# A decoder step on one Trainium2 core: the first half written in plain order, with a recorder in the kernel that orders its instructions and gathers TensorE's side products in 41 bursts

## The chip, the core and the metric

The kernel runs on one core of a Trainium2 chip. A core has TensorE (PE in the profile), VectorE (DVE), ScalarE (ACT), GpSimd (POOL) and SyncE (SP); here SP does little but issue DMAs. Each engine works through its own queue in the order in which the program was written; across engines, semaphores hold an instruction back until its data are there. The metric is the device time of one execution in microseconds, the median of the runs.

## The reference

One layer of a hybrid decoder for a prompt of 512 tokens and 8 samples of 4 tokens, which share all weights (width 1024):

```python
h = rmsnorm(x, norm_mix);  z = h @ w_in          # 3 x 512 columns of attention, 4 x 512 of HGRN
att = dilated_attention(aq, k_all, v_all)        # 8 heads of 64; the samples also read 2048 cached rows
f  = lb + (1 - lb) * sigmoid(hf)                 # HGRN: 4 heads of 128 x 128, a decaying state
S_t = f_t * S_(t-1) + outer(1 - f_t, hi_t);  o_t = S_t^T (silu(hq_t) / sqrt(128))
x += concat(head_rmsnorm(att), head_rmsnorm(o) * silu(hg)) @ w_out
c = rmsnorm(x, norm_cross)                       # cross attention: 4 heads of 128, 256 memory rows
x += softmax((c @ w_cq) k_mem^T / sqrt(128)) v_mem @ w_co
u = rmsnorm(x, norm_ffn)                         # feed forward, 2816 wide, causal convolution of 3
x += (silu(conv3(u @ w_gate)) * (u @ w_up)) @ w_down
y = rmsnorm(x, norm_final)                       # outputs: y, new k/v rows, HGRN states, conv rows, memory k/v
```

All of it is in fp32, for which the kernel uses split products (below).

## The kernel before

**Layout.** Activations lie with the channels on the 128 partitions and the N = 544 tokens (512 of the prompt, then 32 of the samples) in the free dimension, cut as `CUTS` says into 256 and 288. A weight block is 1024 x 128: eight tiles of 128 x 128 that PE holds while the tokens move past.

**Dense passes.** Weights and activations are each split into a high part (`wh`, `xmh`), which has the format fp32r, and the rest (`wl`, `xml`), so each k-tile costs three products: high by high, high by low, low by high. The product is that of L473 in `passes`; a pass over one cut has 24 of them (12 where only four k-tiles are summed, `ps_co`) and fills one of two PSUM banks `dense` (`PD`). ACT makes the high parts of a weight (L381), DVE the low parts (L390), one block ahead. DVE drains the bank (`evac`): `ps_q`, `ps_k`, `ps_v`, `ps_hf`, `ps_hq`, `ps_hg`, `ps_hv` of the input projection in the order `MIX_ORDER`, then `ps_ck` and `ps_cv` for the memory, `ps_wo`, `ps_cq`, `ps_co`.

**Side work.** What lies between dense passes is written as Python generators that a list, `Sides`, holds. A dense pass calls `between()` after half of its products and `sides.pump()` at its end; each pump advances every live generator to its next `yield`. So the hand-placed `yield` statements and the dense passes together set the order on all queues. The generators, with their PE products:
- `decode_attention`, the samples' attention to the 2048 cached rows: `psd` (scores, L719) and `psdo` (values, L770) read tiles `st` that a stream loads from SP's queue into five buffers; `qbd_win` holds the queries, `dpt` the transposed softmax (`psT` at L874). Each group of four products fills 32 of the array's columns and is repeated for four column groups. `pace()` and `PACE` say how many pumps lie between two stream tiles.
- `prompt_attention(p)`, for four pairs of heads: `pst_v` and `pss_v` (v by token, L679 and L684), then for each of four query blocks scores `psS` (L848), softmax on DVE and ACT, transposes `psT`, values `psO`.
- `hgrn(h)`, for four heads: seven levels of a pairwise scheme, in each of which DVE and POOL make operands `kq` from the gates `hf` and their running products `hG` (L922 makes the operand `hq`), and PE multiplies small blocks: `psB` and `psA` (32 x 32 blocks, L935), `psL` (L974, L979); then `psU`, `psu`, `psin` and `pso` for states and outputs, and `psr_hg` (L529) for the norm.
- `memory_in`, `cross_prompt` and `cross_sample` for the cross attention: scores `ps_cp` (L1375), transposes `ps_cpt`, values `ps_cpo`; for the samples `ps_cs`, `ps_cso` and, last, `ps_cos` (L1364), whose drain splits it into the last 32 columns of `coh` and `col`, the inputs of `ps_co`.

The norms between the parts need one product with a matrix of ones, `psr_...` (L529 in `rsqrt_rows`); `psr_cx` gives `r_cx`, by which the drain of `ps_cq` scales. Side products draw on five PSUM banks `aux` (`PX`) and one `dec` (`PDEC`); SBUF operands on a pool of equal slots (`A`).

**The rest.** From the end of `ps_co` on, the feed forward is ordered by `Plan`, a list scheduler in the kernel; the last pass `ps_dz` again by hand.

Of the kernel before, what the change touches and what calls it, by code (L numbers as in the profile page):

```python
# [16 lines left out]
D = 1024  # L17
SEQ = 512
# [39 lines left out]
PACE = (1, 1, 2)  # L58
# [3 lines left out]
HG_WAIT = (2, 0)  # L62
CO_EARLY = (2, 3)
# [17 lines left out]
for _n, _c in (("ident", 128), ("ones", 128), ("blk64", 128), ("dist", 512), ("lnc", 512), ("dbias", NR + 2 * NS),  # L81
               ("mask_a", 96), ("mask_b", 96), ("mask_s", 96), ("batch", NB), ("h8", 8), ("h4", 4), ("sel8", 16),
               ("sel4", 16), ("sel32", 32), ("own", 2)):
    _span(CST_COLS, _n, _c)
# [15 lines left out]
def _constants():  # L100
# [39 lines left out]
    put("batch", ((p[:32, None] // TS) == np.arange(NB)[None, :]).astype(np.float32))  # L140
# [112 lines left out]

@with_exitstack
def tile_decoder_step(ctx: ExitStack, tc: tile.TileContext, xT, memT, kwT, vw, s0, conv_in, mkT, mv, vecs, cst,
                      w_first, w_in, w_out, w_cq, w_ck, w_cv, w_co, w_gate, w_up, w_down,
                      yT, kT_out, vT_out, st_out, conv_out, mkT_out, mv_out, ss_out):
    nc = tc.nc
# [9 lines left out]
    def A(name, shape=None, dt=F32):  # L268
        return act.tile(shape or [128, FW], dt, tag="a", name=name, bufs=NA)

    def R(name):
        return act.tile([128, FW], F32R, tag="a", name=name, bufs=NA)[:, :N]

    def small(name, n=1):
        return one.tile([128, n], F32, tag=f"small{n}", name=name, bufs=16)

    def PD(name):
        return psum.tile([128, 512], F32, tag="dense", name=name, bufs=2)

    def PX(name):  # L280
        return psum.tile([128, 512], F32, tag="aux", name=name, bufs=5)

    def PDEC(name):
        return psum.tile([128, 512], F32, tag="dec", name=name, bufs=1)
# [13 lines left out]
    def step():  # L298
        flush()
        sides.pump()  # L300

    def leave(dst, src, wait=4):

        def gen():
            for _ in range(wait):
                yield
            nc.sync.dma_start(dst, src)
        sides.add(gen())

    vec = one.tile([128, NVEC], F32, name="vec")  # L310
    nc.scalar.dma_start(vec, vecs)
    mid = CST_COLS["dist"][0]
    cs = one.tile([128, mid], F32, name="cs")
    cs2 = strm.tile([128, NCST - mid], F32, name="cs2")
    eps = one.tile([128, 1], F32, name="eps")
# [29 lines left out]
    class Weights:  # L345
# [3 lines left out]
        def load(self, i, now=False):  # L349
            if i < len(specs) and i not in self.raw and (now or i < 3 or i - 3 in self.hl):  # L350
# [4 lines left out]
                if i < down_w:  # L355
                    t = wgt.tile([128, 8, 128], F32, tag="wraw", name=f"wr{i}", bufs=3)
                else:
                    t = A(f"wr{i}", [128, 4, 128])
# [6 lines left out]
        def split(self, i):  # L365
            if i < len(specs) and i not in self.hl:
                self.split_hi(i)
                self.split_lo(i)

        def split_hi(self, i):  # L370
            if i not in self.whole:
# [4 lines left out]
                else:  # L376
                    tiles = [(wgt.tile([128, 8, 128], F32R, tag="whi", name=f"wh{i}", bufs=2),
                              wgt.tile([128, 8, 128], F32R, tag="wlo", name=f"wl{i}", bufs=2), 0, k)]
# [15 lines left out]
        def take(self):  # L394
            self.load(self.i)
            self.split(self.i)
            return self.hl[self.i]

        def ahead(self):

            n = next(i for i in range(self.i, len(specs)) if i not in self.hl)
            for k in range(n + 1):
                self.load(k)
            self.split(n)
            for k in range(n, n + 4):
                self.load(k)

        def advance(self):

            for n in (1, 2, 3):  # L410
                self.load(self.i + n)
            self.split(self.i + 1)
            if self.i + 2 in resident:
                self.split(self.i + 2)
            self.i += 1
# [26 lines left out]
    class Stream:  # L442
# [3 lines left out]
        def load(self):  # L446
            if self.n < len(streams):
                src, w = streams[self.n]
                if self.n < len(streams) - LAST_MV:
                    t = strm.tile([128, 4, 256], F32, tag="st", name=f"st{self.n}", bufs=AHEAD)  # L450
# [18 lines left out]
    def passes(ps, w, xs, n0, n, order, between, first=True, last=True):  # L469
        for at, i in enumerate(order):  # L470
# [4 lines left out]
            if at == (len(order) + 1) // 2 - 1:  # L475
                between()

    def half(w, xs, name, evac, cut, order=None, advance=True):
        n0, n = cut
        ps = PD(f"ps_{name}_{n0}")  # L480

        def between():
            release()
            if advance:
                ws.advance()
            flush()
            if len(xs) > 4:
                sides.pump()

        passes(ps, w, xs, n0, n, order or range(len(xs)), between)  # L490
        evacs.append(lambda: evac(ps, n0, n))
        sides.pump()

    def dense(xs, name, evac, cuts=CUTS, after=None, order=None):
        w = ws.take()
        for c, cut in enumerate(cuts):
            half(w, xs, name, evac, cut, order, c == 0)
        if after is not None:
            pending.append(after)

    def dense_by_half(xs, count, name, evac, after=None, early=(), cuts=CUTS):

        held = []
        for c, cut in enumerate(cuts):
            for m in range(count):
                if c == 0:
                    held.append(ws.take())
                elif early and m in early:
                    ws.ahead()
                half(held[m], xs, f"{name}{m}", lambda ps, n0, n, m=m: evac(m, ps, n0, n), cut, None, c == 0)  # L510
                if after is not None:
                    pending.append(lambda m=m, c=c: after(m, c))
# [12 lines left out]
    def rsqrt_rows(acc, c0, c1, mat, width, r, name):  # L525

        for n0, m in ((c0, c1 - c0),) if c1 - c0 <= 512 else CUTS:
            ps = PX(f"psr_{name}_{n0}")
            nc.tensor.matmul(ps[:, :m], mat, acc[:, n0:n0 + m], start=True, stop=True)  # L529
            yield  # L530
            nc.scalar.activation(r[:, n0:n0 + m], ps[:, :m], AF.Ln, bias=eps, scale=1.0 / width)
            nc.scalar.activation(r[:, n0:n0 + m], r[:, n0:n0 + m], AF.Exp, scale=-0.5)

    def at_once(gen):
        for _ in gen:
            pass
        yield from ()
# [32 lines left out]
    for i in range(2):  # L570
        nc.scalar.dma_start(wf[i], w_first[i])
    nc.scalar.preload_act_table_set(LN_SET)
    for i in range(KT):
        if i == 0:
            x_load(i, 0, 256)
            x_load(i, 256, N)
        else:
            x_load(i, 0, N)
        if i > 1:
            nc.sync.dma_start(wf[i], w_first[i])  # L580
    nc.sync.dma_start(cs, cst[:, :mid])
    for i in range(3):
        ws.load(i)
    nc.sync.dma_start(cs2, cst[:, mid:])
    for _ in range(AHEAD - 1):
        stream.load()
    zero = A("zero")
    nc.vector.memset(zero[:, :128], 0.0)
    warm_up(WARM)

# [9 lines left out]

    for i in range(KT):
        hi, lo = A(f"wfh{i}", [128, 384], F32R), A(f"wfl{i}", [128, 384], F32R)
        for c0, c1 in ((0, 256), (256, N)) if i == 0 else ((0, N),):
            split_into(xs[i], xin[i][:, c0:c1], V("norm_mix", i), c0, c1)
            if c0 == 0:
                nc.scalar.copy(hi, wf[i])
                nc.vector.tensor_tensor(lo, wf[i], hi.bitcast(F32), op=ALU.subtract)
        wf_hl.append((hi, lo))
        if i > 1:
            square(i - 2)  # L610
        if i > 3:
            add_square(i - 3)
    square(KT - 2)
    add_square(KT - 3)
    square(KT - 1)
    add_square(KT - 2)
    add_square(KT - 1)
    ws.split(0)


    lbt = strm.tile([128, 4, 4], F32, name="lbt")
    l0 = vec[:, VEC_COLS["lb0"][0]:VEC_COLS["lb0"][1]]
    l1 = vec[:, VEC_COLS["lb1"][0]:VEC_COLS["lb1"][1]]
# [1333 lines left out]
```

## Time and profile before

| | |
|---|---|
| median of three runs | 864.36 us (864.08 to 864.73) |
| profiled execution | 866.38 us, of which the profile's span is 864.3 |
| TensorE's granted clock, mean | 0.996 of full |
| busy share of PE, DVE, ACT, POOL | 98%, 69%, 46%, 21% |
| DMA, mean over the span | 153 GB/s |
| products on PE | 7578 |

The table's shares are over the whole span. The part that the change rewrites ends at about 478 us; the feed forward fills what is left. PE's busy time is that in which at least one product is under way, and neighbouring products overlap, so a row's duration is more than the distance to the next row's start: what a product costs PE is read from distances between starts.

### The profile page before, as it was taken

To read this page: it belongs to the slowest core of one execution; us is meant where nothing else is said; L and a number is where in the kernel's file an instruction comes from. 1 tells how busy PE (TensorE), PEld (TensorE's weight loads), DVE (VectorE), ACT (ScalarE), POOL (GpSimd) and SP (SyncE) were. 2 spreads that over 40 slices of the span, in tenths; PEclk is the share of its full clock that TensorE was granted. 3 is DMA by queue.
4 is the path that set the end of the run, shared out by engine and by line. 5 is a ranking of instruction groups with operands and counts; after the bars stand their busy time and mean duration, and the time that the engine had idled before them with its cause. 6 is when DMAs were issued, how large, how long until landed. Compare 5 with 4: busy or idle time off the path is not lost.

```text
span 864.3 us, 18847 instructions
## 1 busy us (share of the span) xinstructions
PE 846.4 (98%) x7578; PEld 769.5 (89%) x7578; DVE 598.0 (69%) x1253; ACT 399.8 (46%) x796; POOL 177.2 (21%) x265
## 2 busy tenths in 40 slices
PE   9999999999999999999999999999999999999996
PEld 9997788877777776999888999999999999999995
DVE  6864246776787776546366689886877777777764
ACT  7422125245256334544445554654644544554533
POOL 0230000300300300122222214242322232232113
PEclk9999999999999999999999999999999999999999
DMA  8535875643762785423283227465565555555403
GB/s 303 174 120 145 263 216 177 187 137 101 253 211 76 255 283 186 119 74 110 86 248 103 74 74 175 131 159 135 146 156 138 139 143 151 144 135 134 130 28 104
DMA packets 90759, 132.32 MB, mean 153 GB/s; under 512 B 6064, under 2 KB 60080, under 8 KB 90544
## 3 DMA queue, kind: packets, MB, share of 16 engines
q1 hardware_dynamic: 84480, 120.69, 44.0%
q0 software_dynamic: 5184, 9.44, 6.8%
q8 instruction: 59, 0.97, 0.5%
q10 hardware_dynamic: 1008, 0.99, 0.3%
q14 instruction: 28, 0.23, 0.1%
HBM read 123.03 MB, written 8.07 MB: 152 GB/s over the span
## 4 chain that ended last, share of the span: by engine, by line
PE 83%; DVE 8%; issue 3%; ACT 3%; DMA 1%; POOL 1%; SPq 0%; DVEq 0%; POOLq 0%; ACTq 0%
PE ps_d L473 12%; PE ps_ag L1741 6%; PE ps_au L1741 6%; PE ps_wo L473 6%; PE ps_k L473 3%; PE ps_q L473 3%; PE ps_cg L1741 3%; PE ps_hv L473 3%; PE ps_cu L1741 3%; PE ps_dz L473 3%; PE ps_g L473 2%; PE ps_cq L473 2%; PE ps_hg L473 2%; PE ps_co L473 2%; PE ps_first L643 2%
## 5 line engine op out<-in xcount | busy, mean ns | idle before, releaser
L381 ACT CAST wh<-wr 128x1024 fp32r<-128x1024 f32 (+1 forms) x76 | 65.3, 874 | 82.7 <-PE ps_v L473 20.1
L390 DVE TENSOR_TENSOR wl<-wr,wh 128x1024 fp32r<-128x1024 f32 (+1 forms) x76 | 76.6, 1017 | 37.2 <-ACT wh L381 37.1
L1511 POOL TENSOR_TENSOR up<-up,cv 128x512 f32<-128x512 f32 x22 | 33.2, 1508 | 141.6 <-ACT up L1720 63.9
L956 POOL TENSOR_TENSOR hG<-hG,hf 128x256 f32<-128x256 f32 (+1 forms) x28 | 22.4, 800 | 140.5 <-DVE hf L919 77.3
L1236 DVE TENSOR_TENSOR xr<-xr,ps_d 128x256 f32<-128x256 f32 x80 | 34.7, 434 | 13.6 <-PE ps_d L473 12.7
L1498 DVE SCALAR_TENSOR_TENSOR cv<-ug,vec,cv 128x560 f32<-128x560 f32 x44 | 35.2, 800 | 3.9 <-ACT cv L1489 3.0
L859 ACT ACTIVATE P<-P,mx 128x128 f32<-128x128 f32 (+3 forms) x32 | 18.0, 561 | 39.6 <-DVE mx L858 39.6
L1493 POOL COPY last<-ug 128x2 f32<-128x2 f32 x22 | 11.5, 522 | 98.6 <-ACT ug L1720 80.6
L551 POOL TENSOR_TENSOR acc_cx<-acc_cx,sq_cx 128x256 f32<-128x256 f32 (+1 forms) x14 | 10.8, 771 | 90.1 <-ACT sq_cx L550 90.1
L1489 ACT ACTIVATE cv<-ug,vec 128x560 f32<-128x560 f32 x22 | 18.9, 858 | 16.4 <-DVE ug L1760 11.1
L958 DVE TENSOR_TENSOR hf<-hf 128x256 f32<-128x256 f32 (+1 forms) x28 | 14.5, 519 | 15.1 <-POOL hG L956 14.7
L856 DVE CUSTOM_DVE_ANT_0 P<-psS,bias 128x128 f32<-128x128 f32 (+3 forms) x32 | 15.5, 484 | 7.1 <-PE psS L848 7.0
L719 PE MATMUL psd<-st,qbd_win 128*32 128x224 f32 x256 | 18.7, 365 | 1.5 <-issue 1.5
L473 PE MATMUL ps_co<-coh,wh 128*128 128x256 f32 (+1 forms) x64 | 19.3, 301 | 0.9 <-DVE xr L1236 0.9
L1502 ACT ACTIVATE cv<-cv 128x560 f32<-128x560 f32 x22 | 14.8, 673 | 11.1 <-DVE cv L1498 10.4
L473 PE MATMUL ps_co<-col,wh 128*128 128x256 f32 (+1 forms) x64 | 18.4, 288 | 0.0
L473 PE MATMUL ps_co<-coh,wl 128*128 128x256 f32 (+1 forms) x64 | 18.4, 288 | 0.0
L770 PE MATMUL psdo<-st,dpt 128*32 128x256 f32 x224 | 17.9, 391 | 0.0
L657 DVE TENSOR_TENSOR k<-ps_k,r_mix 128x256 f32<-128x256 f32 (+1 forms) x8 | 3.5, 442 | 20.4 <-PE ps_k L473 20.4
L1754 ACT COPY keptrg<-ps_ag 128x272 f32<-128x272 f32 x9 | 3.5, 385 | 27.7 <-PE ps_ag L1741 27.7
L924 POOL MEMSET hG<- 128x544 f32 x4 | 2.2, 554 | 66.8 <-PE psO L889 33.4
L1687 DVE TENSOR_TENSOR wlu<-wru,whu 128x1024 fp32r<-128x1024 f32 x9 | 12.7, 1409 | 4.5 <-ACT whu L1681 4.5
(2671 smaller groups left out, 3622.3 us busy)
## 6 DMA issues: line engine op xcount, KB each, us to landing
st<-in_kwT SPq DMA_DIRECT2D x32, 448.0 KB, 3.8
st<-in_vw SPq DMA_DIRECT2D x28, 512.0 KB, 4.5
wr<-in_w_in SPq DMA_DIRECT2D x25, 512.0 KB, 4.5
wd<-in_w_down SPq DMA_DIRECT2D x32, 256.0 KB, 2.9
wrg<-in_w_gate SPq DMA_DIRECT2D x9, 512.0 KB, 5.8
wru<-in_w_up SPq DMA_DIRECT2D x9, 512.0 KB, 6.2
st<-in_mkT SPq DMA_DIRECT2D x8, 512.0 KB, 4.7
wr<-in_w_out SPq DMA_DIRECT2D x8, 512.0 KB, 4.0
```

The lines of the kernel that those rows point to most:

```text
L381: nc.scalar.copy(hi[:, :k1 - k0, :], raw[:, k0:k1, :])
L390: nc.vector.tensor_tensor(lo[:, :n, :], raw[:, k0:k1, :], hi[:, :n, :].bitcast(F32), op=ALU.subtract)
L473: nc.tensor.matmul(ps[:, :n], a, b[:, n0:n0 + n], start=(first and at == 0 and j == 0), stop=(last and at == len(order) - 1 and j == 2))
L719: nc.tensor.matmul(ps[32 * b:32 * b + 32, QUART * qu:QUART * qu + QUART], qbd[:, 4 * g + b, p, :], kt[b][:, :QUART], start=p == 0 and qu == 0,
L770: nc.tensor.matmul(po[32 * b:32 * b + 32, 256 * fh:256 * fh + 256], pts[ck // 4][:, at:at + 32], vs[b], start=ck == 0 and fh == 0, stop=ck ...
L859: nc.scalar.activation(pt[:, :nk], pt[:, :nk], AF.Exp, bias=mx, accum_out=den)
L956: nc.gpsimd.tensor_tensor(half(G, 0), half(G, 0), last, op=ALU.mult)
L1236: nc.vector.tensor_tensor(x[m][:, n0:n0 + n], x[m][:, n0:n0 + n], ps[:, :n], op=ALU.add)
L1489: nc.scalar.activation(hid[j][:, :W], ugs[j][:, :W], AF.Identity, bias=V("conv_b", j), scale=V("conv_w0", j))
L1498: nc.vector.scalar_tensor_tensor(hid[j][:, :W], ugs[j][:, i:i + W], V(f"conv_w{i}", j), hid[j][:, :W], op0=ALU.mult, op1=ALU.add)
L1511: nc.gpsimd.tensor_tensor(up[:, :SEQ], up[:, :SEQ], c[:, :SEQ], op=ALU.mult)
L1741: nc.tensor.matmul(ps[:, :HT], l, r, start=first and k == 0 and i == 0, stop=k == 3 and i == 2, skip_group_check=True)
```

## The change

*Recording.* `Tape` stands in for `nc` up to the end of the cross attention. A call such as `nc.vector.tensor_tensor` is not issued but kept, with the tiles and the areas (partitions by columns) that it reads and writes and a rough length worked out from its shape. Consecutive calls on PE become one step; dense products are marked as `main` steps and keep their written order. A step of another engine may not start before a certain dense step ahead of the place where it was written has started (`gate`, `AHEAD`).

*Ordering.* `tape.run()` replays the steps on five modelled engines, three times, each time with the dense steps' starts of the round before as due times (`due`). On ACT, DVE, POOL and SP the step that is due first goes first. On PE side steps are held until one of three things is so: 1 us of ready ones has gathered (`BURST`), 4 us have passed since the first was ready (`PATIENCE`), or no dense step can start. Then all that are ready go one after another, a burst. The start of the kernel keeps its written order.

*Code.* `yield`, `PACE`, `HG_WAIT`, `CO_EARLY`, `between` and the delays in `leave` go away, and `TILES` says how many stream tiles are written at a beat (2, 2, 1). In the prompt attention the query blocks 0 and 1 share one score bank and its softmax steps; the samples' v is transposed into a free part of a `psS` bank. In each HGRN head the samples' rows of v and k are transposed twice, onto two groups of 32 partitions, so that one POOL product replaces two, and `psr_hg` is made for each cut. The three `ps_wo` passes that begin early take two `aux` banks and a dense one instead of three `aux` banks. The feed forward's plan and the last pass are the same.

```diff
-PACE = (1, 1, 2)
+TILES = (2, 2, 1)
...
+    BURST, PATIENCE, SLACK, SPARE, SOON, LEAD = 1.0, 4.0, 12.0, 12, 8.0, 15.0
+    AHEAD = {"SP": 8, "ACT": 5, "DVE": 5, "POOL": 5, "PE": 8}
...
+    def put(self, engine, call, outs, ins, length, lag=None, size=0):
...
+            n = len(self.mains) - self.AHEAD[engine]
...
+            if 0 <= n < len(self.mains) and not main:
+                cur.gate = self.mains[n]
...
+            if free["PE"] <= now + 1e-9:
+                can = [s for s in waiting["PE"] if s.ready <= now + 1e-9 and fits(s)]
+                main = [s for s in can if s.main]
+                side = [s for s in can if not s.main]
+                if side and first is None:
+                    first = now
+                if side and (burst or not main or sum(s.length for s in side) >= self.BURST
+                             or now - first > self.PATIENCE):
+                    if not burst:
+                        free["PE"] = now + 0.1
+                    burst, first = True, None
+                    s = min(side, key=lambda s: (s.begin, s.number))
+                    start(s)
+                    free["PE"] += 0.1
+                    moved = True
+                elif main:
+                    start(main[0])
...
+            elif engine == "ACT":
+                length = 0.05 + 0.00086 * n + 0.19 * ("accum_out" in kw)
...
+            elif engine == "DVE":
+                length = 0.13 + 0.00052 * n if method in ("tensor_scalar", "reciprocal") else 0.08 + 0.00105 * n
...
-    nc = tc.nc
+    nc = tape = Tape(tc.nc)
...
-        def between():
-            release()
-            if advance:
-                ws.advance()
-            flush()
-            if len(xs) > 4:
-                sides.pump()
-
-        passes(ps, w, xs, n0, n, order or range(len(xs)), between)
-        evacs.append(lambda: evac(ps, n0, n))
+        with tape.main():
+            passes(ps, w, xs, n0, n, order or range(len(xs)))
+        evac(ps, n0, n)
         sides.pump()
...
+        groups = ((0, 1), (2,), (3,))
...
+        for i in range(2):
+
+            by_token_s(v, bank["a"][NS * i:NS * i + NS, 384:512])
...
+        nc.gpsimd.tensor_tensor(vm[:2 * NS], vs[:, None, :].to_broadcast([2 * NS, 4, 128]),
+                                C("batch")[:2 * NS, :, None].to_broadcast([2 * NS, 4, 128]), op=ALU.mult)
...
-    dense_by_half(cross_in.hl, XH, "cq", cq_evac, cq_after, early=CO_EARLY)
-    flush()
-    sides.pump()
-    cross[1].append(sides.add(cross_sample()))
-    sides.drain(*cross[0])
+        cross_prompt(h, c)
+
+    dense_by_half(cross_in.hl, XH, "cq", cq_evac, cq_after)
+    cross_sample()
...
-    dense_by_half(co_hl, KT, "co", lambda m, ps, n0, n: add_to(m)(ps, n0, n), co_after)
-    flush()
+    dense_by_half(co_hl, KT, "co", co_evac, co_after)
     r_ffn, ux = ffn_in.r, ffn_in.hl
+    ws.advance()
+    tape.run()
+    nc = tc.nc
```

In the changed kernel every recorded instruction has the line of the recorder, L593, so its rows are told apart by tiles. Three places in PE's order follow; a number behind a tile's name is the program's own, `x4` says that four products of the form follow one another.

The first place is PE's order in the second HGRN head (levels 32 and 64, `psL`) beside the decode attention, the kernel before:

```order
L473 MATMUL ps_hf_0_2143<-xm3h,wl_1975 128x256
L719 MATMUL psd_1925<-st_1926,qbd_win 32x224 x4
L974 MATMUL psL_2171<-kq_32_2137 32x32 x8
L473 MATMUL ps_hf_0_2143<-xm4h,wh_1974 128x256
...
L473 MATMUL ps_hf_0_2143<-xm7h,wl_1975 128x256
L979 MATMUL psL_2171<-kq_64_2180 64x64 x4
L679 MATMUL pst_v_2207<-cs,v_1957 128x128 x4
L684 MATMUL pss_v_2212<-cs,v_1957 32x128
L473 MATMUL ps_hf_256_2214<-xm0h,wh_1974 128x288
```

And with the change (`psA` with `cs,hv` is the doubled transpose):

```order
L593 MATMUL ps_v_256_419<-xm7h,wl_416 128x288
L593 MATMUL psA_381<-kq_16_385 32x32 x16
L593 MATMUL psA_381<-cs,hv_362 32x128 x2
L593 MATMUL psL_388<-kq_32_386 32x32 x8
L593 MATMUL psdo_429<-st_495,dpt_427 32x256 x4
L593 MATMUL psdo_429<-st_501,dpt_427 32x256 x4
L593 MATMUL psL_388<-kq_64_389 64x64 x4
L593 MATMUL pst_v_430<-cs,v_413 128x128 x4
L593 MATMUL psS_436<-cs,v_413 32x128
L593 MATMUL ps_hf_0_481<-xm0h,wh_479 128x256
```

Where two visits half a dense pass apart did this work, one burst between two passes holds it, and PE goes through it without a dense product in between.

The second place is PE's order at the norm ahead of the cross attention, `psr_cx`, before:

```order
L473 MATMUL ps_cq_0_5121<-cx7h,wl_4_4976 128x256
L529 MATMUL psr_cx_5156<-acc_cx,cs 128x256
L473 MATMUL ps_cq_0_5160<-cx0h,wh_0_5047 128x256
...
L473 MATMUL ps_cq_0_5160<-cx3h,wl_0_5048 128x256
L1375 MATMUL ps_cp_5184<-mk_3893,cq_5117 128x256 x2
L473 MATMUL ps_cq_0_5160<-cx4h,wh_4_5049 128x256
```

And now:

```order
L593 MATMUL ps_cq_0_924<-cx7h,wl_4_923 128x256
L593 MATMUL psr_cx_897<-acc_cx,cs 128x256
L593 MATMUL ps_cp_937<-mk_769,cq_909 128x256 x2
L593 MATMUL ps_cp_944<-mk_769,cq_910 128x256 x2
L593 MATMUL ps_cq_0_930<-cx0h,wh_0_926 128x256
```

`psr_cx` stood after the first head of `ps_cq`, with twelve dense products of the next head ahead of `ps_cp`; now it stands after two heads, and two `ps_cp` follow it at once.

The third place is PE's order at `ps_cos`, the last product of the samples' cross attention, before:

```order
L473 MATMUL ps_co_0_5811<-coh_5114,wl_0_5723 128x256
L1364 MATMUL ps_cos<-cs_75,com_5760 128x16 x4
L1364 MATMUL ps_cos<-cs_75,com_5809 128x16 x4
L473 MATMUL ps_co_0_5849<-coh_5108,wh_0_5772 128x256
L473 MATMUL ps_co_0_5849<-col_5109,wh_0_5772 128x256
```

And now:

```order
L593 MATMUL ps_co_0_1078<-coh_906,wl_0_1077 128x256
L593 MATMUL ps_cos<-cs_74,com_1021 128x16 x4
L593 MATMUL ps_cos<-cs_74,com_1023 128x16 x4
L593 MATMUL ps_co_256_1083<-coh_900,wh_0_1028 128x288
L593 MATMUL ps_co_256_1083<-col_901,wh_0_1028 128x288
```

Before, a pass over the first 256 columns followed, which doesn't read the samples' columns; now the first pass over the last 288 columns follows, which does.

1025 lines of the change are left out of this document (626 added, 399 removed).

## The prediction

> **What bounds the kernel now.** I read the page first, for who is busy and for the chain that ended last; then the stretches of time with each engine's busy time, PE's waits, and PE's instructions in order of time around single excursions. An excursion here is a visit that PE makes from the dense passes (`ps_q`, `ps_k`, `ps_wo` and their like) to other products (`psd`, `psB`, `psL`).
>
> ```profile
> span 864.3 us, 18847 instructions
> PE 846.4 (98%) x7578; PEld 769.5 (89%) x7578; DVE 598.0 (69%) x1253; ACT 399.8 (46%) x796; POOL 177.2 (21%) x265
> PE 83%; DVE 8%; issue 3%; ACT 3%; DMA 1%; POOL 1%; SPq 0%; DVEq 0%; POOLq 0%; ACTq 0%
> 250.00:300.00 50.00, 49.80 (x602) 39.18 (x595) 39.19 (x98) 26.82 (x56) 8.87 (x11) 1.00 0.47 153
> ```
>
> PE is busy for 98% of the span and holds 83% of the chain. Even in the 50 us where DVE has most to do (39.19 us, 78%), PE has no more than 0.2 us free. So time can only be won on PE's own queue, and PE's busy time must hold something that isn't work. The waits are few:
>
> ```profile
> PE ps_cv L1222 <- DVE mk L1200: 1.5, 1, 1.5
> PE psd L719 <- issue: 1.5, 1, 1.5
> PE psT L874 <- ACT dpt L758: 1.3, 1, 1.3
> ...
> PE ps_co L473 <- DVE xr L1236: 0.9, 1, 0.9
> PE psA L935 <- DVE kq L954: 0.7, 3, 0.3
> ...
> PE ps_cpt L1388 <- POOL cp L1315: 0.5, 1, 0.5
> ```
>
> In the part that the change rewrites (to about 478 us) they come to 1.5 + 1.5 + 1.3 + 0.9 + 0.7 + 0.5 = 6.4 us.
>
> **What an excursion costs.** Three excursions, in order of time; the first column is the start. The form `128*32` says that a product fills 32 of the array's 128 columns, `128*128` that it fills all.
>
> ```profile
> 72.74 0.28 PE L473 MATMUL ps_k<-xm7h,wl 128*128 128x256 f32 x1
> 72.95 0.59 PE L719 MATMUL psd<-st,qbd_win 128*32 128x224 f32 x8
> 73.47 0.40 PE L473 MATMUL ps_k<-xm0h,wh 128*128 128x288 f32 x1
> 73.71 0.29 PE L473 MATMUL ps_k<-xm0l,wh 128*128 128x288 f32 x1
> 73.84 0.29 PE L473 MATMUL ps_k<-xm0h,wl 128*128 128x288 f32 x1
> ...
> 150.76 0.29 PE L473 MATMUL ps_hv<-xm3h,wl 128*128 128x288 f32 x1
> 150.98 0.46 PE L935 MATMUL psB<-hq,hk 128*32 128x32 f32 x32
> ...
> 151.66 0.29 PE L473 MATMUL ps_hv<-xm4l,wh 128*128 128x288 f32 x1
> ...
> 152.97 0.29 PE L473 MATMUL ps_hv<-xm7h,wl 128*128 128x288 f32 x1
> 153.19 0.59 PE L719 MATMUL psd<-st,qbd_win 128*32 128x224 f32 x8
> 153.59 0.46 PE L935 MATMUL psB<-kq 128*32 128x32 f32 x31
> ...
> 154.27 0.28 PE L473 MATMUL ps_v<-xm0l,wh 128*128 128x256 f32 x1
> ```
>
> Dense products start 0.13 us apart at 288 columns (73.71 to 73.84) and by the same share 0.12 at 256. From the last dense product before an excursion to the second one after it: alone, `psd` takes 73.71 - 72.74 - 0.25 = 0.72 us and `psB` 151.66 - 150.76 - 0.26 = 0.64; both in one excursion 154.27 - 152.97 - 0.25 = 1.05. Joining the two saves 0.72 + 0.64 - 1.05 = 0.31 us. The first dense product after an excursion shows where part of it sits: 0.24 us to its successor instead of 0.13.
>
> An excursion of whole-array products costs nothing beyond its work:
>
> ```profile
> 400.96 0.28 PE L473 MATMUL ps_cq<-cx7h,wl 128*128 128x256 f32 x1
> 401.07 0.60 PE L529 MATMUL psr_cx<-acc_cx,cs 128*128 128x256 f32 x2
> 401.32 0.47 PE L473 MATMUL ps_cq<-cx0h,wh 128*128 128x256 f32 x1
> 401.63 0.28 PE L473 MATMUL ps_cq<-cx0l,wh 128*128 128x256 f32 x1
> ...
> 402.67 0.43 DVE L1408 SCALAR_TENSOR_TENSOR cq<-ps_cq,r_cx 128x256 f32<-128x256 f32 x1 [0.77 <-ACT r_cx L532]
> ...
> 403.15 1.13 PE L1375 MATMUL ps_cp<-mk,cq 128*128 128x256 f32 x4
> ```
>
> 401.63 - 400.96 - 0.24 = 0.43 us for two instructions; the four of `ps_cp` start about as far apart. Overhead 0.
>
> **The change, part by part.** *Fewer excursions.* Counted over the whole order, PE leaves the dense passes 133 times before and 47 times after (six of these lie outside the recorded part). Those that hold a product on part of the array go from 101 to 33. 68 x 0.31 = 21.1 us off PE's path. The dense products, the split casts and the DMA issues (338 rows on SP in both) are as many as before.
>
> The Trainium skill, TensorEngine Tiling (Array Packing), section Key Properties, says that changing the tiling mode drains TensorE; it speaks of every change of mode, and so against bursts that mix modes. By it one counts changes of form, inside bursts too: 252 in the order before, 125 after; at half of 0.31 us each that would be 19.7 us instead of 21.1.
>
> *More small products.* The HGRN heads transpose the sample rows twice (two copies on partitions, so that one GpSimd product replaces two): eight more products.
>
> ```profile
> 165.28 0.28 PE L684 MATMUL psA<-cs,hv 128*32 128x128 f32 x1
> ...
> 165.40 0.27 PE L684 MATMUL psA<-cs,hv 128*32 128x128 f32 x1
> ```
>
> Two instructions 0.12 us apart for each: 8 x 0.24 = 1.9 us more. The shared score banks (blocks 0 and 1) and the fewer scalings touch DVE and ACT alone, which wait for PE here: nothing. Net 19.2 us.
>
> *The old waits go*, since every place is new: 6.4 us, and the lower clock after one of them:
>
> ```profile
> 320.00:326.00 6.00, 4.45 (x22) 1.93 (x21) 2.87 (x7) 1.06 (x4) 0.00 (x0) 0.85 1.03 361
> 326.00:332.00 6.00, 6.00 (x30) 3.94 (x28) 3.91 (x12) 3.58 (x7) 0.00 (x0) 0.87 0.61 224
> ```
>
> The granted clock is 0.85 and 0.87 there, 6 x 0.15 + 6 x 0.13 = 1.7 us lost, behind the 1.5 us wait of `ps_cv`. Together 8.1 us.
>
> *New waits.* The rule that holds side products back until 1 us of them has gathered, 4 us have passed, or no dense product can start, also holds back single ones that others wait for. Two stand in the order. (1) `psr_cx` comes after two heads of `ps_cq` instead of one; both dense banks are then full, and `ps_cp` is next. What ran beside twelve dense products, 401.32 to 403.15, is bare: 1.8 us. (2) `ps_cos` had 24 products of `ps_co` with the first columns behind it; now it is followed by the last columns, which read its result.
>
> ```profile
> 459.63 1.85 PE L1364 MATMUL ps_cos<-cs,com 128*128 128x16 f32 x16
> ...
> 461.34 0.36 PE L473 MATMUL ps_co<-coh,wh 128*128 128x256 f32 x1
> ...
> 461.92 0.16 ACT L1299 CAST coh<-ps_cos 128x32 fp32r<-128x32 f32 x1
> ...
> 462.14 0.19 DVE L1300 TENSOR_TENSOR col<-ps_cos,coh 128x32 fp32r<-128x32 f32 x1
> ```
>
> The low part of the first head is there at 462.33, 1.0 us after `ps_cos` gave way.
>
> (3) Inside bursts a product stands close behind the ACT or DVE step that feeds it. No row has such a burst. From below 0: the recorder starts a step only when its own lengths say that the feeder is done. From above 0.5 us for each of the 33 mixed bursts: the five waits of `psT`, `psA` and `ps_cpt` average 2.5 / 5. I take 0.2, by `psA`'s 0.7 / 3, a chain of the same kind: 33 x 0.2 = 6.6 us (0 to 16.5). (4) Streamed tiles are used up to five in a row, all the buffers there are, with the next five due some 6 us on.
>
> ```profile
> st<-in_kwT SPq DMA_DIRECT2D x32, 448.0 KB, 3.8
> ```
>
> One lands in 3.8 us; five at the 361 GB/s seen at 320 us take 6.4. That just fits; I take one wait as before, 1.5 us (0 to 5). (5) One loss of clock, 1.7 us, since waits as long as the one that brought it come again (0 to 5).
>
> On this last one the Trainium skill, TensorE: Matmul & The Clock Gate, Part 1, says that the clock drops after an idle window of about 3.4 us. Here the trace differs: 1.5 us of waiting were followed by a granted 0.85. By the page no wait of mine would cost clock, and the sum would be 1.7 us lower.
>
> **Sum.** -19.2 - 8.1 + 1.8 + 1.0 + 6.6 + 1.5 + 1.7 = -14.7 us. The profiled execution took 866.4 us (864.3 and 2.1 around it), so 851.7; the median of the runs, 864.4, lies 2.0 lower: 849.7, about 850. From the end of the cross attention on, the plan and its products are the same, so nothing changes there.
>
> **Rivals.** *Feeders late, slower than before.* If in every mixed burst PE waits for its feeder, the gain is eaten at (19.2 + 8.1 - 6.0) / 33 = 0.65 us for each burst. What speaks for it is that the recorder's lengths are rough:
>
> ```profile
> L922 DVE SCALAR_TENSOR_TENSOR hq<-hq,hqs 128x544 f32<-128x544 f32 x4 | 5.7, 1420 | 0.0
> ```
>
> it puts 0.65 us for this step of 1.42. With two waits of 0.5 us in each burst: 864.4 - 27.3 + 6.0 + 33 = 876. Against it: the steps of the heads run ahead of PE on DVE and POOL and need no product, so an error of 0.8 us meets some slack. *DVE falls behind, still faster.* DVE's 78% rises as PE's time shrinks, and the low parts of the weights queue between the heads' steps; with 0.5 us in each burst 10 us more than I sum: 860. *The stream falls behind.* Five buffers drawn at once cost a wait of 1.5 us at about six places, 7.5 us more than summed: 857. *The overhead was cover*: what excursions lost gave DVE its time, and the waits grow by as much: 864. *No new waits* but (1) and (2): 864.4 - 27.3 + 2.8 = 840.
>
> **How the numbers follow.** My forecast (845 to 856) gets 0.52, the clean case at 840 to 844 0.10, DVE behind 0.15, the stream 0.10, cover 0.05, slower 0.08. Times within 0.2% (1.7 us) can hardly be told from no change. Faster: 0.52 + 0.10 + 0.15 + 0.10 = 0.87; same 0.05; slower 0.08. Range 841 to 861: it leaves out most of the slower case and of cover, and half of the clean one.
>
> **What would show it.** In the profile after: PE's busy time to the end of `ps_co` some 20 us less; dense products followed at 0.13 us nearly everywhere; waits of `ps_cp` on DVE near 1.8 us and of `ps_co` on DVE near 1 us; waits inside bursts (`psT`, `psU`, `pso`, `psA`) of 3 to 10 us together; `psd` and `psdo` waiting for DMA under 5 us. I am wrong if joined products don't start closer (gain under 10 us with few waits) or if PE's waits on DVE and ACT exceed 20 us.

## The result and the profile after

The changed kernel takes 839.39 us (838.13 to 841.62) against 864.55 us for the kernel before, measured beside it: a ratio of 0.9709, 95% interval 0.9684 to 0.9733. The forecast was 850, 841 to 861, so the gain was larger than any that the range allowed. The profiled execution has a span of 838.0 us against 864.3, that is 26.3 us less where 14.7 were summed.

The page of the changed kernel, its first lines and the chain:

```profile
span 838.0 us, 18847 instructions
PE 821.8 (98%) x7594; PEld 767.3 (92%) x7594; DVE 590.5 (70%) x1233; ACT 396.4 (47%) x792; POOL 180.1 (21%) x261
PE 88%; DVE 6%; issue 2%; DMA 2%; ACT 1%; POOL 0%; SPq 0%; DVEq 0%; POOLq 0%; ACTq 0%
```

Two stretches of each kernel, the recorded part up to the last product of `ps_co` and the rest (columns: length, then busy time and number of instructions of PE, PEld, DVE, ACT, POOL, the granted clock, DMA), the kernel before first:

```profile
0.00:479.30 479.30, 471.51 (x4622) 397.54 (x4623) 305.76 (x735) 205.86 (x441) 72.84 (x103) 1.00 0.55 173
479.30:864.30 385.00, 374.83 (x2958) 371.97 (x2956) 292.29 (x518) 193.94 (x356) 104.36 (x163) 0.99 0.48 129
```

```profile
0.00:453.20 453.20, 447.18 (x4638) 395.55 (x4639) 297.92 (x715) 202.32 (x436) 76.48 (x99) 1.00 0.57 183
453.20:838.00 384.80, 374.62 (x2958) 371.73 (x2956) 292.59 (x518) 194.10 (x356) 103.62 (x163) 0.99 0.48 129
```

The whole gain lies in the first stretch: PE's busy time falls by 471.51 - 447.18 = 24.3 us, though it runs 16 instructions more, and its idle time from 7.8 to 6.0 us. The forecast had the products and visits 19.2 us down, and waits and clock 4.5 us up.

PE's waits in the changed kernel:

```profile
PE ps_cp L593 <- DVE cq L593: 1.5, 1, 1.5
...
PE ps_cv L593 <- DVE mk L593: 0.7, 1, 0.7
PE psdo L593 <- DMA st<-in_vw: 0.5, 1, 0.5
...
PE psu L593 <- ACT hsm L593: 0.5, 1, 0.5
...
PE pso L593 <- DVE hS L593: 0.3, 1, 0.3
PE ps_co L593 <- ACT coh L593: 0.3, 1, 0.3
```

The number behind the colon is the wait in all, in us. Inside bursts PE waits for a feeder on another engine in two places, `psu` and `pso`, 0.8 us together; the forecast had 6.6. One burst, in PE's order of time:

```profile
44.60 0.30 PE L593 MATMUL ps_q<-xm7h,wl 128*128 128x288 f32 x1
44.82 0.47 PE L593 MATMUL psB<-hq,hk 128*32 128x32 f32 x33
...
45.14 0.82 PE L593 MATMUL psB<-kq 128*32 128x32 f32 x67
45.79 0.96 PE L593 MATMUL psd<-st,qbd_win 128*32 128x224 f32 x16
46.68 0.38 PE L593 MATMUL ps_q<-xm0h,wh 128*128 128x256 f32 x1
46.90 0.28 PE L593 MATMUL ps_q<-xm0l,wh 128*128 128x256 f32 x1
```

Three groups of `psB` and two of `psd`, five visits' worth of work, with one way in and one way out: from 44.60 to 46.90, less the two dense products (0.13 and 0.12), 2.05 us. Alone they would cost 3 x 0.64 + 2 x 0.72 = 3.36 by the prediction's rows.

### The profile page after: what moved, and what is told of

The parts are those of the page before. It is cut to its first block, busy times and chain, and to the rows that moved or that the text cites. A ratio compares the mean times of both kernels' runs of the same rounds, so it can differ in the third digit from the quotient of the medians.

```text
span 838.0 us, 18847 instructions
## 1 busy us (share of the span) xinstructions
PE 821.8 (98%) x7594; PEld 767.3 (92%) x7594; DVE 590.5 (70%) x1233; ACT 396.4 (47%) x792; POOL 180.1 (21%) x261
## 4 chain that ended last, share of the span: by engine, by line
PE 88%; DVE 6%; issue 2%; DMA 2%; ACT 1%; POOL 0%; SPq 0%; DVEq 0%; POOLq 0%; ACTq 0%
PE ps_d L797 12%; PE ps_ag L2039 6%; PE ps_au L2039 6%; PE ps_wo L593 6%; PE ps_co L593 3%; PE ps_cg L2039 3%; PE ps_k L593 3%; PE ps_q L593 3%; PE ps_cq L593 3%; PE ps_hv L593 3%; PE ps_cu L2039 3%; PE ps_g L797 2%; PE ps_hq L593 2%; PE ps_hf L593 2%; PE ps_hg L593 2%; PE ps_dz L797 2%
## 5 line engine op out<-in xcount | busy, mean ns | idle before, releaser
L593 ACT CAST wh<-wr 128x1024 fp32r<-128x1024 f32 (+1 forms) x61 | 53.3, 892 | 109.7 <-PE ps_q L593 20.0
L593 DVE TENSOR_TENSOR wl<-wr,wh 128x1024 fp32r<-128x1024 f32 (+1 forms) x61 | 65.4, 1080 | 9.7 <-ACT wh L593 9.3
L593 POOL TENSOR_TENSOR hG<-hG,hf 128x256 f32<-128x256 f32 (+1 forms) x28 | 25.8, 921 | 192.2 <-DVE hf L593 142.2
L1791 POOL COPY last<-ug 128x2 f32<-128x2 f32 x22 | 9.5, 432 | 97.6 <-ACT ug L2018 79.6
L593 POOL TENSOR_TENSOR acc_cx<-acc_cx,sq_cx 128x256 f32<-128x256 f32 (+1 forms) x14 | 12.4, 890 | 66.5 <-ACT sq_cx L593 66.3
L593 ACT ACTIVATE P<-P,mx 128x128 f32<-128x128 f32 (+3 forms) x32 | 17.6, 551 | 6.1 <-DVE mx L593 6.1
L593 DVE TENSOR_TENSOR xr<-xr,ps_wo 128x256 f32<-128x256 f32 (+1 forms) x16 | 6.8, 436 | 19.2 <-PE ps_wo L593 19.2
L593 PE MATMUL ps_co<-coh,wh 128*128 128x256 f32 (+1 forms) x64 | 19.7, 308 | 0.3 <-ACT coh L593 0.3
L593 PE MATMUL ps_co<-col,wh 128*128 128x256 f32 (+1 forms) x64 | 19.3, 301 | 0.1
L593 PE MATMUL ps_co<-coh,wl 128*128 128x256 f32 (+1 forms) x64 | 19.1, 298 | 0.0
L719 DVE TENSOR_TENSOR wl<-wr,wh 128x512 fp32r<-128x512 f32 (+1 forms) x15 | 14.0, 936 | 6.0 <-ACT wh L710 6.0
L710 ACT CAST wh<-wr 128x512 fp32r<-128x512 f32 (+1 forms) x15 | 12.0, 814 | 9.6 <-PE ps_g L797 4.5
L593 PE MATMUL psd<-st,qbd_win 128*32 128x224 f32 x256 | 16.1, 359 | 0.0
L593 POOL TENSOR_TENSOR acc_ux<-acc_ux,sq_ux 128x256 f32<-128x256 f32 (+1 forms) x14 | 11.2, 798 | 22.2 <-ACT sq_ux L593 21.9
L1985 DVE TENSOR_TENSOR wlg<-wrg,whg 128x1024 fp32r<-128x1024 f32 x9 | 11.0, 1222 | 6.5 <-ACT whg L1979 6.5
```

The lines of the kernel that those rows point to most:

```text
L593: return tape.put(engine, lambda: call(*args, **kw), outs, ins, length, lag, size)
L710: nc.scalar.copy(hi[:, :k1 - k0, :], raw[:, k0:k1, :])
L719: nc.vector.tensor_tensor(lo[:, :n, :], raw[:, k0:k1, :], hi[:, :n, :].bitcast(F32), op=ALU.subtract)
L1791: nc.gpsimd.tensor_copy(last2[:, j, 0:2], ugs[j][:, SEQ:SEQ + 2])
L1985: nc.vector.tensor_tensor(lo, self.raw, self.hi.bitcast(F32), op=ALU.subtract)
```

## Experiments

**What a visit costs.** A block of test products on resident data, between the cross attention and the feed forward (an excerpt of the edit):

```diff
+        for what in ("W", "D", "B", "R", "T", "WW", "DD", "DDDD", "DB", "BDBD", "WD", "WWDD", "WDWD", "RD", "RRDD",
+                     "RDRD", "TD", "TTDD", "TDTD"):
+            ps = PX("pt" + what)
+            for _ in range(8):
+                for k in what:
+                    kinds[k](ps)
+                main()
```

> The changed kernel with a block of test products put between the cross attention and the feed forward (their results are not used; the time as a whole is longer by the block and is not compared). Each visit lies between 12 dense products of 256 columns; W is one fp32 product on the whole array (2 instructions), D four products that fill 32 of 128 columns each (8 instructions), B sixteen 32-column blocks, R one product of 64 rows, T four transposes on the whole array; a tile ptWD is a visit of W then D, eight visits of each. Theory of the prediction (a visit with a part-array product costs 0.31 us once, whatever is in it, a whole-array visit nothing): D alone 0.72 us, DD 1.13, so 0.31 saved; WDWD costs as much as WWDD; WD costs W + D. Rival (each change of array form costs the same, about 0.15 us, inside a visit too): WDWD costs 0.3 us more than WWDD, TDTD 0.3 more than TTDD, RDRD 0.3 more than RRDD; BDBD no more than twice DB less 0.3. Third theory (any change of product, dense to side or back, costs about 0.08 us whatever the form): WW saves 0.1 to 0.2 us against two visits W.

One visit each of `ptWWDD` and `ptWDWD`, in order of time; `ptm` are the dense products:

```profile
663.55 1.03 PE L1718 MATMUL ptWWDD<-cs 128*128 128x256 f32 x4
664.51 0.96 PE L1722 MATMUL ptWWDD<-cs 128*32 128x224 f32 x16
665.40 0.86 PE L1715 MATMUL ptm<-ux1h,ux0h 128*128 128x256 f32 x5
```

```profile
690.54 0.59 PE L1718 MATMUL ptWDWD<-cs 128*128 128x256 f32 x2
691.06 0.59 PE L1722 MATMUL ptWDWD<-cs 128*32 128x224 f32 x8
691.58 0.70 PE L1718 MATMUL ptWDWD<-cs 128*128 128x256 f32 x2
692.21 0.59 PE L1722 MATMUL ptWDWD<-cs 128*32 128x224 f32 x8
692.72 0.84 PE L1715 MATMUL ptm<-ux1h,ux0h 128*128 128x256 f32 x5
```

The same products in another order: 665.40 - 663.55 = 1.85 us against 692.72 - 690.54 = 2.18. A visit's whole cost also holds what it adds to the dense products beside it; by the means of the eight visits, two changes of array form more cost 0.326 us, 0.163 each (`TDTD` against `TTDD` 0.29, `RDRD` against `RRDD` 0.33 for the two). `WW` saves nothing against two `W` (0.86 and 2 x 0.43), `WD` nothing against `W` and `D` (1.15 both), `DD` saves 0.34, `DB` 0.30. So in these pairs the price hangs on the change of form: a visit with products on part of the array pays on the way in, on the way out, and at each change inside.

**The order inside bursts.** One rule more in the recorder, by which a step of the same array form as the last goes first, and its opposite, with `==` in place of `!=` (an excerpt; elsewhere the edit notes each step's forms in `modes`):

```diff
-                    s = min(side, key=lambda s: (s.begin, s.number))
+                    s = min(side, key=lambda s: (s.modes[0] != mode, s.begin, s.number))
+                    mode = s.modes[-1]
```

> The changed kernel, with one rule more in the recorder: among the ready side products of a burst, one of the same array form as the last goes first. Bursts stay at 44 (33 with part-array products) against 43 (33), changes of array form fall from 134 to 91. Theory of the prediction (cost by excursion alone): 839, no change beyond 0.3%. Rival (each change of form costs 0.15 to 0.19 us): 43 x 0.15 to 0.19 = 6.5 to 8.2 us less, 831 to 833.

> The changed kernel, with the opposite rule: among the ready side products of a burst, one of another array form than the last goes first. Bursts stay at 44 (32), changes of array form rise from 134 to 168. Theory of the prediction: 839. Rival: 34 x 0.15 to 0.19 = 5 to 6.5 us more, 844 to 846.

Measured: 831.56 us (ratio 0.961, 0.9588 to 0.9632) with like after like, 845.7 (0.9766, 0.9744 to 0.9789) with unlike after like. PE's busy time, the first row of each page's engines:

```profile
PE 814.7 (98%) x7594; PEld 767.5 (92%) x7594; DVE 590.3 (71%) x1233; ACT 397.9 (48%) x792; POOL 179.5 (22%) x261
```

```profile
PE 828.1 (98%) x7594; PEld 766.4 (91%) x7594; DVE 592.0 (70%) x1233; ACT 399.0 (47%) x792; POOL 180.8 (21%) x261
```

821.8 goes to 814.7 and 828.1, with 44 visits and the same products in both. Between the two lie 77 changes of form and 13.4 us; 1.7 of it is a fall of the clock that the first doesn't have, the rest is 0.15 each. The changed kernel's profiled execution has such a fall too; its one execution with a granted mean of 0.998, like those of the first version, took 838.13 us, 6.6 more than 831.56 for 43 changes, again 0.15 each. The rival's times came out, and the cost by excursion alone is refuted.

**Without gathering.** `BURST` and `PATIENCE` at 0.

> The changed kernel without the rule that holds side products back: they go as soon as they are ready (both the gathered length and the patience at 0). Visits rise from 43 to 57 (33 to 43 with part-array products), changes of form from 134 to 144. Theory of the prediction: 10 x 0.31 = 3.1 us more, less the two waits at the norm and at the end of the samples' cross attention (1.5 + 0.3 us), so 840 to 841. Rival (per change of form): 10 x 0.15 to 0.19 = 1.5 to 1.9 more, less 1.8 of waits, so 839. If gathering were the source of the gain, 850 or more.

841.12 us (0.971, 0.9682 to 0.9737), not to be told from the changed kernel. With 57 visits, against 43 in the changed kernel, it still has less than half of the 129 that the whole recorded part had before: most of the joining doesn't come from the two thresholds. That it comes from letting all ready side products go once PE has left the dense passes is the likely reason, but that rule was not tried by itself.

**The feeders.** Lengths and lags of all engines but PE, as the recorder knows them, times 0.25, then times 0.7:

```diff
+            if engine != "PE":
+                length, lag = 0.25 * length, 0.25 * lag
```

> The changed kernel; the recorder is told a quarter of the lengths and lags of ACT, DVE, POOL and the DMA issues, so it believes the feeders of PE done far too early. Visits 34 (27 with part-array products), changes of array form 131 against 134. Theory of the prediction (side products stand close behind their feeders, and only the recorder's lengths keep PE from waiting): waits inside bursts rise from under 1 us to 27 x 0.2 = 5 us at least, and to 27 x 0.5 = 13 us at most: 844 to 852. Rival (the feeders are done long before, because side steps collect for some 8 us of dense work before a burst, and few steps stand in one burst with their feeders): waits stay under 3 us, time 837 to 841.

> The changed kernel; the recorder is told 0.7 of the lengths and lags of ACT, DVE, POOL and the DMA issues. 43 visits (32 with part-array products), 139 changes of form against 134: 0.8 us more by the price. If a quarter of the lengths cost 78 us by waits (58 us) and lost clock, three in ten too short should cost a part of it: between 3 and 25 us, 843 to 865. If the recorder's lengths have slack (the theory that waits were few since lengths err on the long side): under 3 us, 840 to 842.

917.47 us (1.063, 1.0597 to 1.0663) and 871.01 (1.0079, 1.0065 to 1.0092): both beyond what either theory gave, the first clearly slower than the kernel before, the second 0.8% slower. The largest waits of PE, with a quarter and with 0.7:

```profile
PE pst_hk L595 <- DVE hk L595: 20.0, 3, 8.8
PE psT L595 <- DVE mx L595: 12.9, 3, 6.7
PE psA L595 <- DVE kq L595: 8.4, 6, 2.0
```

```profile
PE pst_hk L595 <- DVE hk L595: 5.0, 3, 2.6
PE psA L595 <- DVE kq L595: 4.7, 4, 1.4
PE psL L595 <- DVE kq L595: 3.6, 4, 1.7
```

These are the feeders that the forecast feared. The few waits of the changed kernel are therefore not slack that is there anyway: the recorder's lengths are long enough as they stand, and three tenths less cost 32 us. About half of that is waiting: PE's idle time, span less busy time, grows from 16.2 to 33.0 us. The rest is PE's busy time, 821.8 to 835.8, at a granted mean of 0.98 instead of 0.996: the clock falls too.

**The two late products.** `psr_cx` and `ps_cos` begin a burst as soon as they are ready:

```diff
-                if side and (burst or not main or sum(s.length for s in side) >= self.BURST
+                if side and (burst or not main or any(n.startswith(URGENT) for s in side for n in s.tiles) or sum(s.length for s in side) >= self.BURST
```

> The changed kernel; the two products that the prediction named as late, the norm's ahead of the cross attention and the last of the samples' cross attention, begin a burst as soon as they are ready. Changes of form stay at 134, visits 44. Prediction's theory of these two waits: 1.5 us before ps_cp and 0.6 us behind ps_cos go, 837.3. If the lower clock after ps_cos (0.55 and 0.60 for 4 us, 1.7 us lost) hangs on that place, it goes too: 835.6. Rival (the waits only move to the next product that is late): 839.

834.9 us (0.9659, 0.9645 to 0.9672), 4.5 us under the changed kernel: both waits, 1.5 and 0.3 us, are gone from PE's list, and the profiled execution has no low clock after `ps_cos`. The changed kernel's has (two stretches of it; the clock is the third number from the end):

```profile
438.00:440.00 2.00, 2.00 (x10) 2.00 (x11) 0.08 (x1) 0.58 (x2) 1.47 (x2) 0.55 0.35 98
440.00:442.00 2.00, 2.00 (x12) 2.00 (x11) 1.19 (x3) 0.87 (x2) 0.00 (x0) 0.60 0.00 0
```

That this loss belongs to the place is not shown. In the run with the first block of test products the recorded part is that of the changed kernel, with the same sixteen `ps_cos` instructions and the same wait of 0.3 us behind them, and the clock stays up:

```profile
438.00:440.00 2.00, 2.00 (x16) 2.00 (x17) 0.48 (x3) 0.64 (x2) 1.49 (x2) 1.00 0.36 98
```

The two waits account for 1.8 of the 4.5 us, and the clock for up to 1.7 in executions that lose it; about 1 us is left open.

**Both together, and more gathering on top.**

> The order by array form (91 changes there, 89 here) together with the two early products. From the 831.6 of the first: 1.5 us of the wait before ps_cp and 2 x 0.16 of changes: 829.8. If the wait only moves: 831.5.

> As the one before, with all norm products early and twice the gathering (2 us and 8 us of patience): 37 visits (25 with part-array products) and 80 changes of form. From 829.8: 9 x 0.16 = 1.4 us less for the changes, 828.4. Rival (longer gathering makes the consumers of side products late, feeders and banks run out): waits grow by more than that, 831 or more.

> Order by array form and the two early products as in the 829.6 version, with 1.5 us gathered and 6 us of patience: 41 visits (27 with part-array products), 85 changes against 89. By the price 4 x 0.16 = 0.6 us less: 829.0. Rival (longer gathering brings waits, as the 2 us version at 833.1 did): 830 to 833.

829.56 us (0.9602, 0.9589 to 0.9615) is the fastest version, 9.8 us under the changed kernel. With 2 us gathered, and all norm products early, it is 833.1 (0.9637, 0.9624 to 0.965); with 1.5 us 837.65 (0.9703, 0.9683 to 0.9722). The rival was right in both: fewer changes, but PE idle for 18.4 and 19.8 us instead of 14.3. The longest wait of the 1.5 us version, whose clock also fell (granted mean 0.994):

```profile
PE psT L600 <- DVE hst L600: 3.2, 2, 3.0
```

**The doubled sample copy.** The four products of `psu` in a head, in the changed kernel, and two of the four before:

```profile
304.25 1.13 PE L593 MATMUL psu<-hvm,hsm 32*128 32x512 f32 x4 [0.48 <-ACT hsm L593]
305.30 1.16 PE L593 MATMUL psU<-hvt,hkt 128*128 128x128 f32 x8
```

```profile
67.09 1.12 PE L1088 MATMUL psu<-hvm,hsm 32*128 32x512 f32 x2
68.14 0.39 PE L473 MATMUL ps_k<-xm0h,wh 128*128 128x256 f32 x1
```

1.05 us from start to the next tile's start for four instructions now, and for two before. The operands lie on two groups of 32 partitions, and the second product uses 32 other rows of the array. To test it, both were read from the first group, so that this version leaves out the states of four of the eight samples:

```diff
-            rows = slice(NS * i, NS * i + NS)
+            rows = slice(0, NS)
             nc.tensor.matmul(pus[i], ks[rows], vm[rows].rearrange("p b v -> p (b v)"), start=True, stop=True)
```

> The changed kernel with one edit: of the two psu products of a HGRN head, the second reads its operands from partitions 0 to 31 like the first, not from 32 to 63 (so the states of four of the eight samples come out of the other four's rows). Order, counts and waits are the same instruction for instruction. Theory found in the two traces (16 psu instructions took 9.0 us before and 4.5 us now, because products on two groups of 32 rows run beside each other): psu takes 9.0 us again, 3.5 to 4.5 us more, 843 to 844. Theory of the prediction (the second copy costs eight transposes and gives PE nothing back): 839.4, the same.

844.03 us (0.9757, 0.9738 to 0.9776), 4.6 us more. All `psu` products of the kernel before, the changed kernel and this one (busy time, mean of one):

```profile
L1088 PE MATMUL psu<-hvm,hsm 32*128 32x512 f32 x16 | 9.0, 640 | 0.0
```

```profile
L593 PE MATMUL psu<-hvm,hsm 32*128 32x512 f32 x16 | 4.5, 638 | 0.5 <-ACT hsm L593 0.5
```

```profile
L593 PE MATMUL psu<-hvm,hsm 32*128 32x512 f32 x16 | 7.9, 611 | 0.5 <-ACT hsm L593 0.5
```

One product lasts as long as ever (611 to 640 ns), but the two run beside each other: 3.4 us between 4.5 and 7.9. The clock fell more often in the profiled execution of this version (granted mean 0.989). The one execution with the changed kernel's 0.996 took 842.92 us, 3.5 more than the changed kernel's median; the rest of the 4.6 us is likely clock.

**The clock.** A second block of test products: `U` a product of 32 rows, then `C`, eight light products of 16 columns each, without a wait, then waits of growing length behind dense work (an excerpt).

```diff
+        for what in ("C", "CC", "CCC", "CCCC"):
+            main(60)
+            ps = PX("pt" + what)
+            for k in what:
+                kinds[k](ps)
+            main(60)
```

> The changed kernel with a second block of test products between the cross attention and the feed forward (results not used, total time not compared). U is a product of 32 rows and 256 columns (like psu), D the four 32-column products. First: by the price of a change of form, 0.16 us, UU saves 2 x 0.16 against two visits U, UDUD costs two changes more than UD twice in one row would, so twice UD less 0.16 (one form met between them instead of the dense products: 6 changes against 5). Then the clock: C is eight products of 16 columns (as ps_cos), up to four in a row between 60 dense products and without a wait; and ptwait, in which a product waits for 1, 2, 3, 4, 6, 8 dependent copies on DVE (some 0.4 us each). If the clock falls for light products alone, CCCC (7 us) brings it below 1; if for waits alone, only the longer ptwait do, from somewhere above the 1.5 us that passed without a loss; if it takes both, neither C nor the short waits show a loss.

`UU` cost 1.24 us against 2 x 0.81, 0.38 less; `UDUD` 2.47 against 2 x 1.33, 0.19 less: 0.19 for each change, somewhat more than with the other forms. Of the clock, stretches during `ptCC` (570.22 to 573.71), during and behind `ptCCC` (587.93 to 593.81), during `ptCCCC` (from 610.53), and behind the longest wait (2.95 us, to 724.55):

```profile
570.00:572.00 2.00, 2.00 (x21) 2.00 (x19) 0.00 (x0) 0.00 (x0) 0.00 (x0) 1.00 0.04 8
572.00:574.00 2.00, 2.00 (x19) 2.00 (x19) 0.00 (x0) 0.00 (x0) 0.00 (x0) 1.00 0.00 0
...
592.00:594.00 2.00, 2.00 (x14) 2.00 (x14) 0.00 (x0) 0.00 (x0) 0.00 (x0) 0.64 0.00 0
594.00:596.00 2.00, 2.00 (x10) 2.00 (x11) 0.00 (x0) 0.00 (x0) 0.00 (x0) 0.50 0.00 0
...
613.00:614.00 1.00, 1.00 (x7) 1.00 (x6) 0.00 (x0) 0.00 (x0) 0.00 (x0) 0.52 0.00 0
...
725.00:727.00 2.00, 2.00 (x14) 1.97 (x13) 0.00 (x0) 0.00 (x0) 0.00 (x0) 0.67 0.00 0
727.00:729.00 2.00, 2.00 (x11) 2.00 (x11) 0.00 (x0) 0.00 (x0) 0.00 (x0) 0.50 0.00 0
```

Light products alone bring the clock down, though PE counts as fully busy. A mean of 0.64 over 2 us is 1.44 us at half clock, so it fell 4.6 us after the start of `CCC`; the 0.52 over 1 us puts the fall at 613.04, 2.5 us after the start of `CCCC`. During `CC`, which lasts 3.5 us, it stayed. So no number of light products can be read from these three tries as a limit. Behind waits of up to 2.28 us the clock stayed, behind the one of 2.95 it fell; each length was tried once. In the kernel before, the low clock at 324 us had stood behind a wait of 1.5 us, and side products (from 322.67 on, `psin` of 32 x 32 among them) came between. Both or either may have brought it: that place was not tried by itself, and the two test-block runs show that the same products at one place, `ps_cos`, need not bring a loss that they brought in another execution.

## Why the prediction was wrong

**The saving by joining: size nearly right, reason wrong.** 68 excursions x 0.31 gave 21.1 us; the runs show 255 - 134 = 121 changes of form x 0.163 = 19.7. The 0.31 was two changes, in and out, measured between two groups of the same form, and the forecast took it for a price of the visit. The Trainium skill, TensorEngine Tiling (Array Packing), section Key Properties, says that a change of the tiling mode drains TensorE. The forecast worked that out too, as 252 - 125 = 127 changes and 19.7 us, and chose the visit; the runs show the change to be the unit. For this change the two come out alike, by luck, which hid the mistake. For the order inside bursts they don't, and there the price by visit would have missed the whole gain.

**The doubled copy: wrong sign.** It stood as +1.9 us for eight transposes. Left out was that `psu` then runs on two row groups at once: -3.4 us with the order held fixed (4.5 less between the rows of the two kernels). The Trainium skill, TensorEngine Tiling (Array Packing), section Key Properties, says that different tiles can work in parallel. The trace agrees (1.05 us for two products and for one). What the eight transposes cost by themselves was not measured.

**The new waits: the step that failed most.** The in-burst waits, 33 x 0.2 = 6.6 us, measured 0.8: the value was taken from `psA`'s three old waits, which came from a hand-placed order, and carried over to an order whose rule is to start nothing before its feeder is done by the recorder's lengths (with 0.7 of these `psA` alone waits 4.7 us). Of the others, `psr_cx` to `ps_cp` was forecast at 1.8 and is 1.5, and the stream 1.5 and is 0.5. The end of `ps_cos` was forecast at 1.0 and is 0.3 in the list of waits; some 0.4 more lies in PE's busy time, as the second product of the next pass starts 0.49 us after the first (437.35 to 437.84) instead of 0.13. One old wait stayed in part, that of `ps_cv` for `mk`, with 0.7 us. Waits and clock were to be 4.5 us worse on balance; PE's idle time is 1.8 us better.

**The loss of clock: its size right, its place by luck.** It came as 2 x 0.45 + 2 x 0.40 = 1.7 us, at another place than the wait it was tied to, and it doesn't come in every execution of the same order. The sum also seems to take the loss of the kernel before off twice: once as a term of 1.7 us, and once in the 2.0 us from the profiled execution, whose granted mean is 0.996, to the median. Of the 34 executions of that kernel beside the experiments 27 have 0.997 or 0.998; for the first three the clock is not on record.

**The sum.** The forecast fell 26.3 - 14.7 = 11.6 us short in the profiled execution. The in-burst waits are 5.8 of that, and the doubled copy up to 5.3. From the runs, changes -19.7, `psu` -3.4 and idle time -1.8 make 24.9 of the 26.3 us, before what the extra transposes take back; the low clock is in both executions, 1.7 us each. With 4.5 for `psu` it would be 26.0. Up to some three us thus stay open. In the visits of the kernel before there are delays that the list of waits doesn't show (the four `ps_cpt` transposes at 409.90 us cost 0.9 us beside their wait of 0.5, four transposes in the test block 0.44).

**The rivals.** The case without new waits, at 840 with a chance of 0.10, gave the time, though in part by luck: its two late products are there, but so are other waits and a low clock, and it had no gain from `psu`. That DVE or the stream falls behind did not occur. The case of late feeders is real as a mechanism, with its `pst_hk`, `psA` and `psL`, but only where the recorder's lengths are too short.

## What to carry to other kernels

Count the changes of TensorE's array form on a queue, inside bursts as well as at their ends, and order what is ready so that like follows like: here 0.163 us each, and 6.6 us for one rule in the scheduler between executions with the same granted clock (7.8 between the medians). Where an order is planned with rough lengths, let them be long rather than short, and let a single product that others wait for go ahead of any rule that gathers. When an edit spreads operands over more partitions, look at what then runs side by side before pricing the copies.

## What the runs showed of the hardware

- A change of array form costs 0.14 to 0.19 us of TensorE's time in the pairs tried: between 128 x 32 products and whole-array products 0.163, products of 64 rows 0.165, of 32 rows 0.19, whole-array transposes 0.14. A visit of whole-array fp32 products between fp32r ones costs nothing beyond its work (two of them 0.86 us, one 0.43).
- Two products on 32 different rows of the array run beside each other: 16 instructions in 4.5 us instead of the 9.0 of the kernel before, and 7.9 where both read the same rows.
- The granted clock falls to 0.5 after light products, without any idle time in the profile, as well as after a wait: 24 products of 16 columns (48 instructions, 5.9 us) brought it down, 16 (3.5 us) did not, and in a third try it fell 2.5 us after the first. Eight such products (1.85 us) and a wait of 0.3 us were followed by a low clock in one execution of the changed kernel's order and not in two others.
- By the Trainium skill, TensorE: Matmul & The Clock Gate, Part 1, the clock goes down after an idle window of about 3.4 us. No wait tried here was that long: the clock stayed behind one of 2.28 us, and fell already behind one of 2.95.
